# A decoder layer on one core: weight-quadrant sums by accumulating DMA, the last adaLN split moved into the down projection, token sums on VectorE

## The chip, the cores and the metric

One Trainium2 chip, of which the program uses one core. The metric is device time of one execution in microseconds (us). Engines are named as in the profile: PE is TensorE (matmuls), PEld its weight loads, DVE is VectorE, ACT is ScalarE, POOL is GpSimd, SP is SyncE, which here only issues DMAs. ACT and POOL issue DMAs too, each on a queue of its own.

## The reference

One trunk layer for 512 tokens of width 2048, all in float32:

```python
mod = silu(c) @ w_ada + b_ada            # six vectors: sh_a, sc_a, gt_a, sh_f, sc_f, gt_f
h = rmsnorm(x, g_pre_attn) * (1 + sc_a) + sh_a
qa, ka, va, qb, kb, vb = split(h @ w_in, 6)
oa = rmsnorm(dilated_mixture_attention(rope(qa) * s, rope(ka), va), g_out_a)
ob = rmsnorm(differential_attention(rope(qb) * s, rope(kb), vb, lam), g_subln_b) * (1 - lambda_init)
x = x + gt_a * rmsnorm(concat(oa, ob) @ w_out, g_post_attn)
h = rmsnorm(x, g_pre_ffn) * (1 + sc_f) + sh_f
f = (silu(h @ w_gate) * (h @ w_up)) @ w_down        # width 5632
x = x + gt_f * rmsnorm(f, g_post_ffn)
```

`c` is one vector, so each of the six `w_ada` parts (2048 x 2048, 16 MB) is read once and reduced against `silu(c)`: pure transfer, and a product with a sum on VectorE.

## The kernel before, in words

**Steps.** The whole program is a list of steps, `steps`. A step is one weight tile of 128 x 1024 float32 (512 KB) and the matmuls that use it. To keep float32 accuracy the tile is split into a high part `w_hi` (ACT, L1530, `do_hi`) and a low part `w_lo` (DVE, L1539, `do_lo`), the activations likewise, and each product is three matmuls of 128x512 (L282 to L284: high x high, high x low, low x high). Splits run two steps ahead of the matmuls (`LA = 2`): in step i, ACT makes the high part of step i+2 and DVE its low part. There are three buffers for each. What else is due in a step hangs in tables keyed by step number (`start_ev`, `pe_ev`, `mid_ev`, `post_ev`, `post_late`, `post_end`, and `aux` for extra loads); the loop at the end emits them in that order, and every engine and every queue then runs its own instructions strictly in that order. Nothing reorders them afterwards.

**Loads.** SP loads weight tiles into a ring of four buffers, `w_raw` (`NRAW = 4`, `pump_loads`, L1515). The ring is shared: tiles of the steps and "aux" tiles of `w_ada` (`in_adar`) go through it in order of use, and a load is issued when the tile four places earlier has been used.

**Stages.** The input projection with attention; the output projection (64 steps from `W0`, 12 matmuls each, `in_wout`); block 0 of the FFN (32 steps from `F0`, `in_wgu`); blocks 1 to 10 of the FFN (280 steps from `F1`); the down projection (88 steps from `D0`, 24 matmuls each, `in_wdown`, with the activations read back from DRAM).

**The adaLN parts.** `w_ada` parts n = 2, 0, 1, 3 are each 32 tiles of 512 KB. A planner loop walks the steps, adds up estimated DVE and DMA time, and hangs as many tiles on each step as it thinks fit. `ada_use` does the work: one DVE instruction with an accumulated sum (L228) against `silu(c)`. Part 3 (`gt_f`) is needed last, at the end of the down projection, through `ada_row` (a transpose on PE, a small DMA out, and a broadcast back into `GTG[1]`).

**Blocks 1 to 10: seven products for eight.** For a block the gate and up weights form a 2 x 2 matrix of quadrants q0 to q3 (gate/up by halves of the input width), 4 tiles each. With sums of token halves ("E" tiles) and sums of quadrants, seven products of four steps replace eight: slots m1 (q0), P (q0+q2), Q (q0+q2+q3), Y2 (q3), R (q2+q3), m2 (q1), T (the rest). Step numbers inside a block run from 0 to 27: P at 4 to 7, Q at 8 to 11, Y2 at 12 to 15, R at 16 to 19, m2 at 20 to 23, T at 24 to 27. `w_load` (SP) loads every quadrant once, 16 tiles a block, and `w_sums` (DVE, L1379) makes the sums in place, 16 tile sums a block, four steps ahead of use (`SL = 4`). Twelve buffers hold these tiles; `w_free` and `w_sums` give them back.

**Token sums.** In block 0, from step F0+16, `e_load` (SP) reads eight pieces of the normalised activations back from DRAM; `e_sums` makes four sums of 128x256 for each on POOL (L1233 to L1236), and `e_split` copies the result to a high part on ACT (L1247) and the rest to a low part on DVE (L1248). The same piece of the program also ends the output projection's second half of tokens: residual, norm, and transposes back (`wo_res`, `wo_norm`, `h2_tr`, L1178 on PE).

**The end.** `d_evac` takes the down projection's sums out of PSUM: a square with a sum on ACT (L1476) and the product with `GTG[1]` on DVE (L1477).

The two lines around which the change turns are the planner's list and the place of its left-overs:

```python
ada_todo = [(n, ch, hf) for n in (2, 0, 1, 3) for ch in range(16) for hf in range(2)]
...
for i, (n, ch, hf) in enumerate(ada_todo):
    aux[D0 + 2 + i].append((adar[n, ch, hf], ada_use(n, ch, hf)))
```

Of the kernel before, what the change touches and what calls it, by code (L numbers as in the profile page):

```python
# [5 lines left out]
F = mybir.dt.float32  # L6
# [28 lines left out]
def body(tc, t):  # L35
# [5 lines left out]
    with ctx:  # L41
# [874 lines left out]
        rawt = {}  # L916
# [4 lines left out]
        for g in range(1, 11):  # L921
            for name, a, bk in SLOTS:
                for j in range(4):
# [11 lines left out]
                    quad = {"m1": 0, "P": 0, "Q": 0, "T": 0, "m2": 1, "R": 2, "Y2": 3}[name]  # L935
                    add("s", None, mm, prov=lambda g=g, quad=quad, j=j: rawt[g, quad, j])
# [95 lines left out]
        ada_todo = [(n, ch, hf) for n in (2, 0, 1, 3) for ch in range(16) for hf in range(2)]  # L1032
# [18 lines left out]
        for i in range(W0 + 60):  # L1051
# [24 lines left out]
            while ada_todo and (ada_todo[0][0] == 3 or i < W0 + 46) and i >= 1 and t_dve + 1.14 <= t_end + (M_ADA if i < W0 else M_ADAW) and \  # L1076
# [153 lines left out]
        def e_sums(j):  # L1230
            h, e = v3(esum[j], 4), stage.get()
            o = v3(e, 4)
            pool.tensor_tensor(o[:, 0, :], h[:, 2, :], h[:, 3, :], op=OP.subtract)  # L1233
            pool.tensor_tensor(o[:, 1, :], o[:, 0, :], h[:, 0, :], op=OP.subtract)
            pool.tensor_tensor(o[:, 2, :], h[:, 0, :], h[:, 2, :], op=OP.subtract)
            pool.tensor_tensor(o[:, 3, :], h[:, 1, :], o[:, 1, :], op=OP.add)  # L1236
            stage.add(esum[j])
            esum[j] = e

        def e_split(j):  # L1240
# [4 lines left out]
            o = v3(esum[j], 4)  # L1245
# [82 lines left out]
        post_ev[F0 + 8].append(lambda: stage_alloc(0))  # L1328
# [14 lines left out]
        SL = 4  # L1343
# [412 lines left out]
```

## Time and profile before

| | us |
|---|---|
| median of 3 runs | 2279.52 |
| range of the runs | 2278.01 to 2283.3 |
| the profiled execution, its own time | 2278.92 |
| its span, first to last instruction | 2277.1 |
| PE busy | 2222.8 (98%) |
| DVE busy | 1594.9 (70%) |
| ACT busy | 1032.8 (45%) |
| POOL busy | 74.2 (3%) |
| mean granted TensorE clock | 0.992 |

A matmul of 128x512 is shown with 0.39 us, but in a full stretch one starts every 0.227 us: they overlap in the pipeline. So a gap of up to some 0.16 us between two of them does not show as idle time, and time lost in a stage is better read from the number of matmuls in a stretch than from PE's busy share. The profiled execution is 0.6 us below the median of the runs.

### The profile page before, as it was taken

How to read it: one execution, taken by the hardware profiler on the slowest of the kernel's cores; microseconds unless marked ns; L12 is line 12 of the kernel's file. 1: busy time of each engine (PE TensorE's matmuls, PEld its weight loads, DVE VectorE, ACT ScalarE, POOL GpSimd, SP SyncE). 2: the span in 40 equal slices, each digit the busy share in tenths (PEclk: the TensorE clock that was granted, in tenths of full speed). 3: DMA queues.
4: the chain of work that ended last, by engine and by line, in shares of the span. 5: the costliest groups of instructions: out<-in, count | busy, mean ns of one | idle time of the engine just before them, and what ended most of it. 6: DMA issues, size and time to landing. Idle time of an engine off the chain costs nothing.

```text
span 2277.1 us, 26712 instructions
## 1 busy us (share of the span) xinstructions
PE 2222.8 (98%) x10012; PEld 1808.3 (79%) x10012; DVE 1594.9 (70%) x2201; ACT 1032.8 (45%) x1507; POOL 74.2 (3%) x68
## 2 busy tenths in 40 slices
PE   7999999999999888999999999999999999999998
PEld 6888777778887666778888888888888888888886
DVE  6987877776777786777778777777777644444445
ACT  5443344444435454644454444444444433333432
POOL 0000000000001000150000000000000000000000
PEclk8999999999999999999999999999999999999999
DMA  9796544456778888864224323422432656655564
GB/s 370 296 332 213 157 139 166 145 163 192 222 260 278 300 295 300 276 240 147 94 93 157 130 98 115 157 93 93 157 140 80 252 194 211 195 189 200 189 218 185
DMA packets 124802, 440.11 MB, mean 193 GB/s; under 512 B 13792, under 2 KB 25344, under 8 KB 118272
## 3 DMA queue, kind: packets, MB, share of 16 engines
q1 hardware_dynamic: 105936, 406.14, 51.8%
q10 hardware_dynamic: 18736, 32.27, 4.4%
q8 instruction: 78, 1.28, 0.2%
q14 instruction: 52, 0.43, 0.1%
HBM read 404.25 MB, written 25.18 MB: 189 GB/s over the span
## 4 chain that ended last, share of the span: by engine, by line
PE 83%; DMA 6%; DVE 6%; issue 2%; ACT 2%; POOL 1%; ACTq 0%; SPq 0%; DVEq 0%; POOLq 0%
PE b L283 21%; PE b L284 21%; PE b L282 20%; PE b L277 5%; PE b L279 5%; PE b L278 5%; DMA w_raw<-in_wout 5%; DVE w_lo L1539 2%; PE b L507 2%; PE b L545 1%; ACT w_hi L1530 1%; DVE w_raw L228 1%; PE b L1262 1%; PE b L500 1%; PE b L529 1%
## 5 line engine op out<-in xcount | busy, mean ns | idle before, releaser
L1539 DVE TENSOR_TENSOR w_lo<-w_raw,w_hi 128x1024 fp32r<-128x1024 f32 x264 | 325.6, 1237 | 312.9 <-ACT w_hi L1530 312.5
L1530 ACT ACTIVATE w_hi<-w_raw 128x1024 fp32r<-128x1024 f32 x264 | 278.7, 1057 | 461.6 <-PE b L284 309.2
L283 PE MATMUL b<-w_lo,h 128*128 128x512 f32 x864 | 338.6, 392 | 7.7 <-DVE w_lo L1539 6.2
L282 PE MATMUL b<-w_hi,h 128*128 128x512 f32 x864 | 342.1, 396 | 0.4 <-ACT xT L212 0.4
L284 PE MATMUL b<-w_hi,h 128*128 128x512 f32 x864 | 337.1, 390 | 0.0
L1530 ACT ACTIVATE w_hi<-raw 128x1024 fp32r<-128x1024 f32 x196 | 208.1, 1062 | 268.9 <-PE b L284 244.3
L1539 DVE TENSOR_TENSOR w_lo<-raw,w_hi 128x1024 fp32r<-128x1024 f32 x196 | 240.1, 1229 | 103.1 <-ACT w_hi L1530 102.6
L284 PE MATMUL b<-w_hi,acthl 128*128 128x512 f32 x704 | 274.0, 389 | 0.4 <-DVE acthl L972 0.4
L282 PE MATMUL b<-w_hi,acthl 128*128 128x512 f32 x704 | 274.1, 389 | 0.0
L283 PE MATMUL b<-w_lo,acthl 128*128 128x512 f32 x704 | 273.9, 389 | 0.0
L282 PE MATMUL b<-w_hi,e 128*128 128x512 f32 x640 | 249.7, 390 | 0.0
L283 PE MATMUL b<-w_lo,e 128*128 128x512 f32 x640 | 249.0, 389 | 0.0
L284 PE MATMUL b<-w_hi,e 128*128 128x512 f32 x640 | 249.0, 389 | 0.0
L277 PE MATMUL b<-h,w_hi 128*128 128x512 f32 x512 | 213.4, 417 | 0.0
L278 PE MATMUL b<-h,w_hi 128*128 128x512 f32 x512 | 201.0, 393 | 1.6 <-DVE h L273 1.6
L279 PE MATMUL b<-h,w_lo 128*128 128x512 f32 x512 | 201.6, 394 | 0.0
L283 PEld LDWEIGHTS b<-w_lo,h 128*128 128x128 f32 x864 | 162.3, 188 | 48.1 <-DVE w_lo L1539 15.0
L282 PEld LDWEIGHTS b<-w_hi,h 128*128 128x128 f32 x864 | 162.2, 188 | 37.5 <-issue 3.7
L284 PEld LDWEIGHTS b<-w_hi,h 128*128 128x128 f32 x864 | 162.2, 188 | 33.6
L284 PEld LDWEIGHTS b<-w_hi,acthl 128*128 128x128 f32 x704 | 132.1, 188 | 28.0 <-DVE acthl L972 0.8
L282 PEld LDWEIGHTS b<-w_hi,acthl 128*128 128x128 f32 x704 | 132.1, 188 | 27.8 <-DVE stage L1314 0.2
L283 PEld LDWEIGHTS b<-w_lo,acthl 128*128 128x128 f32 x704 | 132.2, 188 | 27.3
(246 smaller groups left out, 3262.8 us busy)
## 6 DMA issues: line engine op xcount, KB each, us to landing
w_raw<-in_adar SPq DMA_DIRECT2D x128, 512.0 KB, 4.6
raw<-in_wgu SPq DMA_DIRECT2D x109, 512.0 KB, 4.5
w_raw<-in_win SPq DMA_DIRECT2D x107, 512.0 KB, 5.0
actf<-act2d SPq DMA_DIRECT2D x88, 512.0 KB, 4.7
w_raw<-in_wdown SPq DMA_DIRECT2D x88, 512.0 KB, 3.5
w_raw<-in_wout SPq DMA_DIRECT2D x64, 512.0 KB, 4.9
w_lent<-in_wgu SPq DMA_DIRECT2D x51, 512.0 KB, 4.6
ada<-in_ada SPq DMA_DIRECT2D x21, 1024.0 KB, 9.2
```

Of the source, the lines that this page charges most:

```text
L228: dve.scalar_tensor_tensor(w, w, 1.0, silu_h[half], op0=OP.mult, op1=OP.mult, accum_out=dst)
L277: pe.matmul(ps, whi, ahi, start=start, stop=False, **kw)
L278: pe.matmul(ps, whi, alo, start=False, stop=False, **kw)
L279: pe.matmul(ps, wlo, ahi, start=False, stop=stop, **kw)
L282: pe.matmul(ps, ahi, whi, start=start, stop=False, **kw)
L283: pe.matmul(ps, ahi, wlo, start=False, stop=False, **kw)
L284: pe.matmul(ps, alo, whi, start=False, stop=stop, **kw)
L500: pe.matmul(sc[:, r], qk[:, i, qs], qk[:, i + 1, :N], start=True, stop=True)
L507: pe.matmul(sc[:, :N], qk[k, 2 * m, qs], qk[k, 2 * m + 1, :N], start=True, stop=True)
L529: pe.transpose(tr[:, j, :], misc["p"][:, n % 2, 128 * j:128 * j + 128], ident)
L1530: act.activation(hi, raw, AF.Copy)
L1539: dve.tensor_tensor(lo, raw, hi.bitcast(F), op=OP.subtract)
```

## The change

Six things, all in the tables and helpers named above:

1. **Quadrant sums.** `w_load` now loads five sets a block: q2 as "P", q0 as "B11", q3 as "B22", q2 again as "R", q1 as "B21", 20 tiles. `w_sums` makes three of the four sums with DMAs issued by POOL that add what they read to what lies in the buffer (`accum_op=OP.add`): P += q0, later P += q1, and R += q3, 12 a block. One sum, P += B22, stays on DVE, 4 a block. Buffers are given back after m1, Y2, R, m2 and T.
2. **The last adaLN part.** The planner no longer places part 3. All its 32 tiles hang on down-projection steps D0+2 to D0+33. `ada_row(3)` moves from D0+18..20 to D0+34..36, and the spill of `silu(c)` from W0+62 to W0+50.
3. **Its consumer.** `d_evac` of the first column group copies instead of multiplying by `GTG[1]`; `d_gain` multiplies later, at D0+46, 48, 50, 52.
4. **Token sums.** `e_sums` runs on DVE instead of POOL, with the high-part copy on ACT right behind it; the low part (`e_lo`) is made one step later. The eight pieces stand 2.5 steps apart instead of 2, from F0+17 to F0+34.
5. **Transposes** (`h2_tr`) of both token halves run one step later.
6. **Buffers.** The first stage buffers of block 0 are taken at F0+2 instead of F0+8, and three of the four lent buffers at F1-4 instead of F1-3.

```diff
@@ planner
-        ada_todo = [(n, ch, hf) for n in (2, 0, 1, 3) for ch in range(16) for hf in range(2)]
+        ada_todo = [(n, ch, hf) for n in (2, 0, 1) for ch in range(16) for hf in range(2)]
...
-        assert len(ada_todo) <= 16 and all(a[0] == 3 for a in ada_todo), ada_todo
-        start_ev[W0 + 62].append(lambda: [act.dma_start(silud[:, 1024 * h:1024 * h + 1024], silu_h[h]) for h in range(2)])
+        assert not ada_todo
+        ada_todo = [(3, ch, hf) for ch in range(16) for hf in range(2)]
+        start_ev[W0 + 50].append(lambda: [act.dma_start(silud[:, 1024 * h:1024 * h + 1024], silu_h[h]) for h in range(2)])
...
-        row = ada_row(3, 7)
-        post_late[D0 + 18].append(row[0])
-        mid_ev[D0 + 19].insert(0, row[1])
-        start_ev[D0 + 20].append(row[2])
+        row = ada_row(3, 3)
+        post_late[D0 + 34].append(row[0])
+        mid_ev[D0 + 35].insert(0, row[1])
+        start_ev[D0 + 36].append(row[2])
@@ token sums
-            pool.tensor_tensor(o[:, 0, :], h[:, 2, :], h[:, 3, :], op=OP.subtract)
...
+            dve.tensor_tensor(o[:, 0, :], h[:, 2, :], h[:, 3, :], op=OP.subtract)
...
+            act.activation(SA["E", 0, j // 2][:, j % 2], o, AF.Copy)
+        def e_lo(j):
             hi, lo = SA["E", 0, j // 2][:, j % 2], SA["E", 1, j // 2][:, j % 2]
-            act.activation(hi, o, AF.Copy)
-            dve.tensor_tensor(lo, o, hi.bitcast(F), op=OP.subtract)
+            dve.tensor_tensor(lo, v3(esum[j], 4), hi.bitcast(F), op=OP.subtract)
...
         for j in range(8):
-            post_ev[F0 + 16 + 2 * j].append(lambda j=j: e_load(j))
-            post_ev[F0 + 17 + 2 * j].append(lambda j=j: e_sums(j))
-            post_ev[F0 + 19 + 2 * j].append(lambda j=j: e_split(j))
+            at = F0 + 17 + 5 * j // 2
+            start_ev[at - 3].append(lambda j=j: e_load(j))
+            post_end[at].append(lambda j=j: e_sums(j))
+            post_end[at + 1].append(lambda j=j: e_lo(j))
@@ quadrant sums and loads
-        def w_sums(e):
-            p = e + SL
...
-            ab = {"P": (0, 2), "Q": (0, 3), "R": (2, 3), "T": (0, 1)}.get(name)
...
-            dve.tensor_tensor(x, x, y, op=OP.add)
...
-        wloads = sorted((F1 + 28 * (g - 1) + {0: -2, 2: 0, 3: 4, 1: 18}[q] + j, g, q, j)
-                        for g in range(1, 11) for q in range(4) for j in range(4))
-        LEAD = 4
+        wloads = sorted((F1 + 28 * (g - 1) + at + j, F1 + 28 * (g - 1) + end + j, g, n, q, j)
+                        for g in range(1, 11) for n, q, at, end in
+                        (("P", 2, -8, -5), ("B11", 0, -6, -4), ("B22", 3, -1, 2), ("R", 2, 6, 9), ("B21", 1, 14, 16))
+                        for j in range(4))
+        USE.update({"m1": "B11", "P": "P", "Q": "P", "Y2": "B22", "R": "R", "m2": "B21", "T": "P"})
...
+        def w_sums(e):
+            for g in range(1, 11):
+                k = e - F1 - 28 * (g - 1)
+                for j in range(4):
+                    if k - j == -4:
+                        pool.dma_start(rawt[g, "P", j], wgu[g, 0, j], accum_op=OP.add)
+                    elif k - j == 4:
+                        dve.tensor_tensor(rawt[g, "P", j], rawt[g, "P", j], rawt[g, "B22", j], op=OP.add)
+                    elif k - j == 7:
+                        pool.dma_start(rawt[g, "P", j], wgu[g, 1, j], accum_op=OP.add)
+                    elif k - j == 10:
+                        pool.dma_start(rawt[g, "R", j], wgu[g, 3, j], accum_op=OP.add)
...
@@ transposes (both token halves)
-            pe_ev[b1 + 8 + i].append((0, a))
-            post_ev[b1 + 8 + i].append(b)
+            pe_ev[b1 + 9 + i].append((0, a))
+            post_ev[b1 + 9 + i].append(b)
...
@@ end
-            dve.tensor_tensor(u, ps, GTG[1][:, cg, :], op=OP.mult)
+            if cg == 0:
+                dve.tensor_copy(u, ps)
+            else:
+                dve.tensor_tensor(u, ps, GTG[1][:, cg, :], op=OP.mult)
+        def d_gain(tb):
+            u = HF["du", tb][:, 0, :]
+            dve.tensor_tensor(u, u, GTG[1][:, 0, :], op=OP.mult)
...
```

**SP's queue, output projection.** `in_wout` is a step's weight tile, `in_adar` a tile of `w_ada`, `in_xtok` the tokens for the residual. Before, around the first pair of token loads:

```order
L1515 DMA w_raw<-in_adar 128x1024
L1515 DMA w_raw<-in_wout 128x1024 x2
L1128 DMA x_5898<-in_xtok 128x2048
L1128 DMA x_5900<-in_xtok 128x2048
L1515 DMA w_raw<-in_adar 128x1024
L1515 DMA w_raw<-in_wout 128x1024
```

Now, from the last `in_adar` of this stage on:

```order
L1522 DMA w_raw<-in_adar 128x1024
L1522 DMA w_raw<-in_wout 128x1024 x9
L1128 DMA x_5889<-in_xtok 128x2048
L1128 DMA x_5891<-in_xtok 128x2048
L1522 DMA w_raw<-in_wout 128x1024 x32
L1128 DMA x_6642<-in_xtok 128x2048
L1128 DMA x_6644<-in_xtok 128x2048
L1522 DMA w_raw<-in_wout 128x1024 x6
```

Of the 49 tiles of `w_ada` that stood between the first and the last `in_wout` load, 19 are left, all ahead of the 18th `in_wout` load; the 30 behind it, two for every three weight tiles, are gone to the down projection.

**POOL's queue, one block of the FFN, now** (L1395 is P += q1, L1397 is R += q3, L1391 is the next block's P += q0; the buffers are `raw` and `w_lent`). Before, POOL had nothing here:

```order
L1395 DMA raw_7682<-in_wgu 128x1024
L1395 DMA raw_7683<-in_wgu 128x1024
L1395 DMA w_lent<-in_wgu 128x1024
L1397 DMA raw_7683<-in_wgu 128x1024
L1395 DMA w_lent<-in_wgu 128x1024
L1397 DMA raw_7419<-in_wgu 128x1024
L1397 DMA w_lent<-in_wgu 128x1024
L1397 DMA raw_7682<-in_wgu 128x1024
L1391 DMA raw_7683<-in_wgu 128x1024
```

The first of R's four sums stands fourth, behind three of P's; the last stands eighth.

**DVE, block 0, two pieces of token sums, now** (`w_lo` is a step's low part, L1233 to L1236 the sums that were POOL's, L1246 the low part of a token sum):

```order
L1546 TENSOR_TENSOR w_lo<-w_raw,w_hi 128x1024
L1233 TENSOR_TENSOR stage_7304<-stage_6928 128x256
L1234 TENSOR_TENSOR stage_7304<-stage_7304,stage_6928 128x256
L1235 TENSOR_TENSOR stage_7304<-stage_6928 128x256
L1236 TENSOR_TENSOR stage_7304<-stage_6928,stage_7304 128x256
L1546 TENSOR_TENSOR w_lo<-w_raw,w_hi 128x1024
L1246 TENSOR_TENSOR e_7337<-stage_7304,e_7333 128x1024
L1546 TENSOR_TENSOR w_lo<-w_raw,w_hi 128x1024
L1233 TENSOR_TENSOR stage_7304<-stageb 128x256
```

The four sums now stand between two low parts; before, DVE had only `w_lo` (two in a row) and the low part of a token sum here.

## Rows read from the trace of the kernel before

**Rows 1.** The page, part 1: busy time, share of the span, instructions.

```profile
PE 2222.8 (98%) x10012; PEld 1808.3 (79%) x10012; DVE 1594.9 (70%) x2201; ACT 1032.8 (45%) x1507; POOL 74.2 (3%) x68
```

**Rows 2.** Stretches: us; busy (x) of PE, PEld, DVE, ACT, POOL; PEclk, DMA share, GB/s.

```profile
676.80:734.80 58.00, 55.29 (x290) 46.25 (x289) 45.62 (x82) 30.16 (x66) 7.29 (x4) 1.00 0.83 281
734.80:903.70 168.90, 146.36 (x609) 113.61 (x608) 124.38 (x175) 77.52 (x117) 3.69 (x4) 0.96 0.86 306
903.70:950.00 46.30, 46.20 (x217) 37.40 (x216) 38.48 (x55) 35.12 (x55) 4.65 (x4) 1.00 0.77 257
950.00:1004.00 54.00, 47.78 (x209) 37.98 (x209) 34.16 (x28) 26.10 (x28) 33.02 (x30) 1.00 0.76 285
1004.00:1787.20 783.20, 781.84 (x3514) 645.75 (x3514) 600.69 (x543) 377.99 (x429) 4.69 (x3) 1.00 0.35 121
1787.20:2268.50 481.30, 480.93 (x2130) 397.78 (x2128) 226.29 (x211) 185.37 (x209) 1.66 (x3) 1.00 0.61 205
```

**Rows 3.** The same view, a stretch inside the down projection.

```profile
1860.00:2260.00 400.00, 399.63 (x1764) 330.48 (x1763) 182.06 (x165) 154.61 (x173) 0.55 (x1) 1.00 0.58 196
```

**Rows 4.** Waits, 734 to 904 us: total us, times, longest us.

```profile
ACT w_hi L1530 <- DMA w_raw<-in_wout: 69.3, 32, 6.7
...
PE b L283 <- DVE w_lo L1539: 12.7, 15, 2.5
...
PE b L1178 <- DVE x L1156: 3.7, 1, 3.7
```

**Rows 5.** Chain that ended last, 735 to 770 us: start us, us, what.

```profile
756.04 8.35 DMA w_raw<-in_wout
...
766.84 4.61 DMA w_raw<-in_adar
```

**Rows 6.** Groups of instructions, 950 to 1009 us (second half of block 0).

```profile
L1539 DVE TENSOR_TENSOR w_lo<-w_raw,w_hi 128x1024 fp32r<-128x1024 f32 x16 | 23.0, 1454 | 4.0 <-ACT w_hi L1530 4.0
...
L1247 ACT ACTIVATE e<-stage 128x1024 fp32r<-128x1024 f32 x7 | 7.4, 1058 | 13.0 <-POOL stage L1236 13.0
...
L1233 POOL TENSOR_TENSOR stage<-stageb 128x256 f32<-128x256 f32 x3 | 4.9, 1641 | 2.7 <-DMA stageb<-h2d 2.7
...
L1235 POOL TENSOR_TENSOR stageb<-stage 128x256 f32<-128x256 f32 x1 | 0.7, 744 | 0.0
```

**Rows 7.** The same view, whole span.

```profile
L1530 ACT ACTIVATE w_hi<-raw 128x1024 fp32r<-128x1024 f32 x196 | 208.1, 1062 | 268.9 <-PE b L284 244.3 <-DVE w_lo L1539 6.9 <-DVE stage L1318 5.0
...
L1379 DVE TENSOR_TENSOR raw<-raw,raw 128x1024 f32<-128x1024 f32 x62 | 76.0, 1226 | 0.0
...
L843 DVE TENSOR_TENSOR mixlo<-mixT,mixhi 128x256 fp32r<-128x256 f32 x32 | 12.1, 421 | 13.3 <-ACT mixhi L842 13.3
```

**Rows 8.** Timeline, ACT, then DVE, block 0: start us, us, what.

```profile
963.69 1.06 ACT L1247 ACTIVATE e<-stageb 128x1024 fp32r<-128x1024 f32 x1 [0.62 <-POOL stage L1233]
964.65 1.04 ACT L1530 ACTIVATE w_hi<-w_raw 128x1024 fp32r<-128x1024 f32 x1
...
968.89 1.21 DVE L1248 TENSOR_TENSOR e<-stage,e 128x1024 fp32r<-128x1024 f32 x1
970.03 1.21 DVE L1539 TENSOR_TENSOR w_lo<-w_raw,w_hi 128x1024 fp32r<-128x1024 f32 x1
```

**Rows 9.** Chain that ended last, blocks 1 and 2.

```profile
1075.32 1.24 DVE stage L1306
...
1153.70 1.24 DVE stage L1306
```

**Rows 10.** DMA issues: count, KB each, median us from issue to landing.

```profile
w_raw<-in_adar SPq DMA_DIRECT2D x128, 512.0 KB, 4.6
raw<-in_wgu SPq DMA_DIRECT2D x109, 512.0 KB, 4.5
...
ada<-in_ada SPq DMA_DIRECT2D x21, 1024.0 KB, 9.2
```

**Rows 11.** DMA rate in 40 slices of 735 to 904 us.

```profile
GB/s 355 219 305 143 382 420 410 281 282 309 283 333 257 253 288 205 354 354 391 340 241 267 279 306 320 320 190 247 378 172 276 259 425 411 273 305 315 334 381 359
```

More of the change, by code (lines that the diff above doesn't have):

```diff
@@ L934, in mm @@
                                  first and k == 0, j == 3 and k == 1, skip_group_check=True)
-                    quad = {"m1": 0, "P": 0, "Q": 0, "T": 0, "m2": 1, "R": 2, "Y2": 3}[name]
-                    add("s", None, mm, prov=lambda g=g, quad=quad, j=j: rawt[g, quad, j])
+                    add("s", None, mm, prov=lambda g=g, name=name, j=j: rawt[g, USE[name], j])
         D0 = len(steps)
@@ L1075, in body @@
             t_dma = max(t_dma, t_pe) + 1.45 * (1 + len(aux[i]))
-            while ada_todo and (ada_todo[0][0] == 3 or i < W0 + 46) and i >= 1 and t_dve + 1.14 <= t_end + (M_ADA if i < W0 else M_ADAW) and \
+            while ada_todo and i < W0 + 46 and i >= 1 and t_dve + 1.14 <= t_end + (M_ADA if i < W0 else M_ADAW) and \
                     t_dma + 1.45 <= t_end + M_DMA and len(aux[i]) < NAUX:
@@ L1232, in e_sums @@
             o = v3(e, 4)
-            pool.tensor_tensor(o[:, 0, :], h[:, 2, :], h[:, 3, :], op=OP.subtract)
-            pool.tensor_tensor(o[:, 1, :], o[:, 0, :], h[:, 0, :], op=OP.subtract)
-            pool.tensor_tensor(o[:, 2, :], h[:, 0, :], h[:, 2, :], op=OP.subtract)
-            pool.tensor_tensor(o[:, 3, :], h[:, 1, :], o[:, 1, :], op=OP.add)
+            dve.tensor_tensor(o[:, 0, :], h[:, 2, :], h[:, 3, :], op=OP.subtract)
+            dve.tensor_tensor(o[:, 1, :], o[:, 0, :], h[:, 0, :], op=OP.subtract)
+            dve.tensor_tensor(o[:, 2, :], h[:, 0, :], h[:, 2, :], op=OP.subtract)
+            dve.tensor_tensor(o[:, 3, :], h[:, 1, :], o[:, 1, :], op=OP.add)
             stage.add(esum[j])
             esum[j] = e
-        def e_split(j):
             if ("E", 0, 0) not in SA:
@@ L1389, in w_load @@
+        USE.update({"m1": "B11", "P": "P", "Q": "P", "Y2": "B22", "R": "R", "m2": "B21", "T": "P"})
         def w_load(e):
-            while wloads and wloads[0][0] - LEAD <= e:
-                need_, g, q, j = wloads[0]
-                p = rawp.get(("R2", "R8", "P1", "P4") if g == 10 and q < 2 else None)
+            while wloads and wloads[0][0] <= e:
+                at, end, g, n, q, j = wloads[0]
+                p = rawp.get(("R2", "R8", "P1", "P4") if g == 10 and n in ("P", "B21") else None)
@@ L1393, in w_load @@
                 if p is None:
-                    assert need_ > e + 1, (need_, e, g, q, j)
+                    assert end > e, (e, wloads[0])
                     return
                 wloads.pop(0)
-                rawp_of[g, q, j] = p
-                rawt[g, q, j] = p[1]
+                rawp_of[g, n, j] = p
+                rawt[g, n, j] = p[1]
                 sync.dma_start(p[1], wgu[g, q, j])
+        def w_sums(e):
[10 more added lines that the diff above has]
+                        pool.dma_start(rawt[g, "R", j], wgu[g, 3, j], accum_op=OP.add)
@@ L1406, in w_free, with raw_lend @@
                 k, j = divmod(r, 4)
-                if SLOTS[k][0] in ("R", "T"):
-                    rawp.add(rawp_of.pop((g + 1, 2 if SLOTS[k][0] == "R" else 0, j)))
+                if SLOTS[k][0] not in ("P", "Q"):
+                    rawp.add(rawp_of.pop((g + 1, USE[SLOTS[k][0]], j)))
         actu = []
-        def raw_lend():
-            for _ in range(4):
+        def raw_lend(n):
+            for _ in range(n):
                 w = wp.tile([128, 1024], F, name="w_lent", tag="raw", bufs=NRAW)
@@ L1461, in body @@
             a, b = h2_tr(1, i, 4 + i % 4)
-            pe_ev[b1 + 7 + i].append((0, a))
-            post_ev[b1 + 7 + i].append(b)
+            pe_ev[b1 + 8 + i].append((0, a))
+            post_ev[b1 + 8 + i].append(b)
         out = t["out"]
@@ L1642, in body @@
             k = i - D0 - 66
+            if i - D0 in (46, 48, 50, 52):
+                d_gain((i - D0 - 46) // 2)
             if k in (10, 12, 14, 16):
```

20 lines of the change are left out of this document (4 added, 16 removed).

## Prediction

> **What bounds the kernel now.** I read the busy times first: PE is busy for 98% of the span [rows 1], so only a stretch in which PE waits can give time back. Next the table of stretches, one per stage [rows 2]. In the down projection PE starts 1764 instructions in 400.0 us, one per 0.227 us [rows 3]; that is my price of a 128x512 matmul at the full clock (granted 1.00, the 2.4 GHz level). A step of 12 matmuls then takes 2.72 us, a step of 24 takes 5.45. In block 0 the stretch 903.7 to 950 holds 217 instructions, 30 of them short transposes (of 128 columns): 187 x 0.227 = 42.4, and 3.9 us for the 30, 0.13 each. With these two prices I ask of each stretch what PE alone would need:
>
> - 734.8 to 903.7 (output projection, steps 16 to 63): 577 x 0.227 + 32 x 0.13 = 135.1 of 168.9 us. **34 us lost**, and the mean clock is 0.96.
> - 676.8 to 734.8 (steps 0 to 15): by the same count some 4 us lost.
> - 950 to 1004 (rest of block 0, 8 transposes): 201 x 0.227 + 1.0 = 46.6 of 54.0. **7 us lost.**
> - 1004 to 1787 (blocks 1 to 10): a block takes 78.4 us from one L1306 to the same one of the next block [rows 9]. Its matmuls take 336 x 0.227 = 76.3, its 16 transposes 2.1: under 1 us a block is lost.
> - The down projection: nothing, 481 us for 88 x 5.45 = 480.
>
> So two stretches can give, by 34 and 7 us. In the first, the waits say what ends last [rows 4]: ACT waited 69.3 us in 32 pieces for `in_wout` tiles, and PE then for the parts made from them. The chain shows the same, tile after tile landing 4.6 to 8.4 us after its issue [rows 5]. The ring of four buffers is the bound: a load is issued when the tile four places earlier is used, and here five tiles in every three steps go through it. DMA engines are not full (share 0.86, 306 GB/s [rows 2], with slices of 420 [rows 11]).
>
> **The change, part by part.**
>
> *30 `w_ada` tiles leave the output projection.* From step 15 on one tile per step goes through the ring instead of 5/3. The ring turned over 113 tiles in the 226.9 us of this stage, 2.0 us each; one per 2.72 us is within that. VectorE also loses 30 products of 1.2 us. What is then late next: residual and norm around step 39, where PE once waited 3.7 us for L1156 [rows 4]. The same work for the other token half ran in block 0, 903.7 to 950, without `w_ada` tiles, and there PE was busy for 46.2 of 46.3 us [rows 2]; the change also gives it one more step. I keep 1.5 us of the 34 as a remainder: **-32.5 us.** Ends: -34 (all of it) and -22.5 (only what PE's busy column shows idle, 168.9 - 146.4).
>
> *The 32 tiles in the down projection.* Per step of 5.45 us the ring now takes two tiles, 2.73 us each, against 2.0 shown possible. VectorE adds 1.2 us to the 2.6 it is busy per step (226 us in 88 steps), ACT nothing. DMA goes from 205 GB/s to 205 + 0.52 MB / 5.45 us = 301 for 174 us, under the 306 of the stage they leave. Cover: the split runs two steps ahead, so a tile may be 5 us late before PE sees it. **0.** Upper end: 1.1 us a tile, what each costs now (34 / 30), 36 us in all. If the cover went, PE would wait for `w_lo`.
>
> *Gate row, gains, spill.* The row moves 16 steps; a bank of the first column group is free by then. Four gains of 128x512 on VectorE are hidden by its idle half. The spill of `silu(c)` on ACT's queue stands ahead of nothing that is due. 0.
>
> *Token sums on VectorE.* POOL needed 1.6 us for a sum beside VectorE and 0.74 alone; `w_lo` took 1454 ns on average there, against 1226 for a like instruction in the later blocks [rows 7]; ACT waited 13.0 us for POOL [rows 6]. Now a piece costs VectorE 4 x 0.42 [rows 7] and no waiting for POOL. But in both queues new waits stand in line: ACT's copy waits for the sums, and the next `w_hi` stands behind it. One round is `w_lo` 1.23, sums 1.7, copy 1.06, `w_hi` 1.06 [rows 7], `w_lo` 1.23 = 6.3 us, in 2.5 steps = 6.8 us: it fits, but where a piece comes after two steps (5.45 us), or where block 0's two sigmoids (step 25) fall in, the part is late. Followed piece by piece with the full durations I lose 13.6 us, with starts as close as the trace shows them in a row (0.96 us on ACT, 1.14 on DVE [rows 8]) 6.6 us, against 7 now. **0**, ends -4 and +6.
>
> *Quadrant sums by DMA.* VectorE loses 12 of 16 sums of 1.23 us a block [rows 7], worth nothing here: PE did not wait for it. L1306 waits for ACT's sigmoid, which stands behind `w_hi`, not for a sum. The price is in what replaces them. A block now moves 32 tile transfers instead of 16: 16.8 MB in 78.4 us, 214 GB/s instead of 107, plus 13 GB/s of stores; under 306. 12 of them add to their destination, and the trace has no such transfer. Two of the three have time: the next block's P has 10 steps, T some 15. R is the tight one. POOL's first sum into P waits until VectorE has made Q's first `w_lo` (end of step 6); R's last stands eighth in POOL's queue, and must have landed 2.3 us (1.06 + 1.23) before step 19: 12 x 2.72 - 2.3 = 30 us for eight. Less 5 us of DMA time for the four B21 loads behind them, **3.2 us each** may be spent. Bounds for one: 1.25 us (0.52 MB at the 420 GB/s of a slice [rows 11]) and 4.5 us (a plain load from issue to landing [rows 10], if they ran strictly one after another); the far end is 9.2, the landing of a transfer of twice the bytes in the crowded start [rows 10]. The program lets eight be in flight, so I take the near end: hidden, **0**.
> The Trainium skill (Collectives: The Full Stack, "The bandwidth ceiling") says that a reducing transfer is slower not for its add but because it reads two sources, which halves its rate. No row here shows it; by it one would take 2.5 us, an estimate, still under 3.2, and the sum stays, with a third of the margin.
>
> **Sum.** 2278.9 (the profiled execution) - 32.5 + 0 = 2246.4; that execution lies 0.6 below the median, so **2247 us**.
>
> **Rivals.**
>
> 1. *The accumulating DMA is late (slower).* Place: R's sums, steps 16 to 19 of each block: ACT's `w_hi` waits for a POOL transfer, PE for both. For it: there is no row for such a transfer, eight stand in one queue, and the eighth is due. Against: 30 us of cover, and DMA engines with a share of 0.35 there [rows 2]. Over 3.2 us each, a block loses 8x + 5 - 30.4 us; the whole gain is spent at x = 3.6. At 4.5 us: 10.6 us a block, 106 in all: 2247 + 106 = **2353**.
> 2. *The stall moves with the tiles.* The down projection waits for its ring as the output projection did: half of 36 us comes back, **2265**; all of it, 2283, no change. Against it: two tiles in 5.45 us where the ring did 2.7.
> 3. *The output projection does not let go.* Another chain (norms, PSUM evacuation) takes the place of the ring and only the lower end is gained: 2278.9 - 22.5 + 0.6 = **2257**. Against it: the clean stretch 903.7 to 950.
>
> **How the numbers follow.** My forecast 0.61, its own range 2236 to 2256. Rival 3, 0.10; rival 2, 0.10, of it 0.04 without change; rival 1, 0.19. A measurement of this kernel can tell about 0.2% (4.6 us) from no change. Faster: 0.61 + 0.10 + 0.06 = 0.77; same 0.04; slower 0.19. The range has to hold 8 in 10. Low end: all 34, the 7 of block 0 and 3 in blocks 1 to 10 gained: 2278.9 - 44 = 2235. High end: rivals 2 and 3 whole, and rival 1's start: 2285. Beyond it lies most of rival 1.
>
> **What would show it.** Right: the output projection from its step 16 takes 136 us, no ACT wait for `in_wout` over a few us, clock 1.00 there; L1306 to the next still 78.4 us; the down projection 481 us with L228 in it and no PE wait; block 0 near 100 us, ACT waiting for the sums on DVE instead of POOL. Wrong: ACT waits for a DMA `raw<-in_wgu` issued by POOL around R, a block well over 79 us, or landing times of these transfers over some 10 us.

## The result and the profile after

| | before | after |
|---|---|---|
| median, us | 2278.77 (4 runs, 2276.07 to 2283.3) | 2250.15 (4 runs, 2247.42 to 2250.81) |
| ratio, 95% interval | | 0.987 [0.9852, 0.9888] |
| span of the profiled execution | 2277.1 | 2248.8 |

The change is faster by 28.6 us (2247 was forecast, within 2235 to 2285). Where it comes from is read stage by stage, from the start of a stage's first matmul to the start of the next stage's first (the down projection: to the start of its last), as the timelines of TensorE give them. All kernels of this study stand in one table (us; "a later block" is the usual period of blocks 2 to 10):

| kernel | output projection | block 0 | block 1 | a later block | down projection | median |
|---|---|---|---|---|---|---|
| before | 226.9 | 100.4 | 78.4 | 78.4 | 480.3 | 2278.8 |
| **after** | **192.6** | **99.2** | **86.0** | **78.3** | **480.4** | **2250.2** |
| 1 adaLN part alone | 194.1 | 100.5 | 78.3 | 78.4 | 480.3 | 2245.9 |
| 2 quadrant sums back on DVE | 192.6 | 97.3 | 84.0 | 78.4 | 480.6 | 2248.8 |
| 3 transfers without the add | 193.2 | 96.2 | 83.0 | 78.3 | 480.3 | 2245.3 |
| 4 q1's two steps later | 191.7 | 97.4 | 85.6 | 78.3 | 480.3 | 2250.6 |
| 5 R's first | 192.5 | 97.2 | 85.8 | 78.3 | 480.3 | 2249.2 |
| 6 R's twice | 193.3 | 97.5 | 98.4 | 90.6 (mean) | 480.3 | 2371.5 |
| 7 two adaLN tiles a step | 193.1 | 97.3 | 87.4 | 78.3 | 480.3 | 2249.3 |
| 8 = 2, sums on POOL, copy two steps on | 192.5 | 92.7 | 78.3 | 78.4 | 480.3 | 2237.9 |
| 9 = 2, sums on DVE, copy two steps on | 194.0 | 92.7 | 78.6 | 78.4 | 480.3 | 2237.1 |
| 10 = after, copy two steps on | 193.1 | 92.7 | 84.0 | 78.3 | 480.3 | 2242.1 |
| 11 = 1, with 30 products | 200.5 | 100.6 | 78.4 | 78.4 | 480.3 | 2253.4 |
| 12 = before, part 3 in half tiles | 218.2 | 100.2 | 78.4 | 78.4 | 480.3 | 2269.6 |

Each row is one profiled execution, and a stage whose code is the same in two kernels can differ between them: the output projection takes 191.7 to 194.1 us in the changed kernel and experiments 1 to 10, and experiment 7, which differs from the changed kernel in the down projection alone, has 97.3 and 87.4 for blocks 0 and 1 instead of 99.2 and 86.0. Differences of a stage under some 2 us are not read as effects.

So 34.3 us were gained in the output projection and 1.2 in block 0, and 7.6 given back in block 1. The busy times of the page, part 1, against [rows 1]:

```profile
PE 2214.3 (98%) x10012; PEld 1807.1 (80%) x10012; DVE 1471.7 (65%) x2117; ACT 1030.5 (46%) x1507; POOL 142.7 (6%) x156
```

VectorE lost 123 us of work, net, mostly quadrant sums, and that is no measure of anything: the later blocks that they left take 78.3 us instead of 78.4. The stretches of the changed kernel (columns as in [rows 2]): output projection steps 16 to 63, block 0 by halves, block 1, blocks 2 to 10, down projection.

```profile
734.30:868.90 134.60, 134.60 (x610) 111.06 (x609) 89.69 (x115) 77.38 (x117) 3.69 (x4) 1.00 0.79 268
868.90:917.10 48.20, 48.11 (x225) 38.85 (x224) 38.86 (x56) 35.55 (x55) 4.66 (x4) 1.00 0.75 244
917.10:968.10 51.00, 48.26 (x201) 38.85 (x200) 36.54 (x50) 23.08 (x25) 2.80 (x3) 0.93 0.84 287
968.10:1054.10 86.00, 80.62 (x354) 64.14 (x352) 51.79 (x53) 38.69 (x43) 11.49 (x13) 1.00 0.91 264
1054.10:1759.10 705.00, 704.22 (x3171) 581.81 (x3169) 421.68 (x380) 340.28 (x390) 91.87 (x104) 1.00 0.81 223
1759.10:2239.70 480.60, 480.23 (x2124) 397.10 (x2122) 262.20 (x274) 184.80 (x209) 1.66 (x3) 1.00 0.70 238
```

In the first row PE is busy for all of 134.60 us at a granted clock of 1.00, where [rows 2] had 146.36 of 168.90 at 0.96. The third and fourth are what is left: PE idle for 2.7 and 5.4 us, the clock at 0.93 in the third. In blocks 2 to 10 the DMA share rose from 0.35 to 0.81 and PE did not notice. The waits of the first stretch, against [rows 4] (L1537 is now the line of `w_hi`, L1546 that of `w_lo`):

```profile
ACT w_hi L1537 <- PE b L284: 41.2, 34, 1.7
...
ACT w_hi L1537 <- DMA w_raw<-in_wout: 9.6, 4, 3.6
...
PEld b L283 <- DVE w_lo L1546: 0.4, 2, 0.2
```

ACT's wait for `in_wout` is down from 69.3 us to 9.6; it now waits for PE to free a buffer, so PE is the bound.

What the new transfers cost stands in two places. The page, part 3 (queue; packets, MB, share of 16 engines' span), and the instructions of L1397, the sums into R (first who waited for them, then issue to landing):

```profile
q1 hardware_dynamic: 111696, 427.11, 54.6%
q0 software_dynamic: 17280, 62.92, 14.7%
```

```profile
  ACT w_hi L1537: 67.9, 26
...
DMA to landing us min/median/max: 8.3/15.4/22.0
```

q0 holds the 120 accumulating transfers: 14.7% of 2248.8 us over 120 is 2.75 us of all 16 engines for each 512 KB. R's forty, which stand behind others, land after 15.4 us in the median, and ACT waited 67.9 us for them. Block 4 shows how near that came (timelines of ACT, DVE, PEld and PE; R's last tile):

```profile
1261.17 1.06 ACT L1537 ACTIVATE w_hi<-w_lent 128x1024 fp32r<-128x1024 f32 x1 [2.75 <-DMA w_lent<-in_wgu]
```

```profile
1262.26 1.23 DVE L1546 TENSOR_TENSOR w_lo<-w_lent,w_hi 128x1024 fp32r<-128x1024 f32 x1 [2.59 <-ACT w_hi L1537]
```

```profile
1263.54 0.19 PEld L283 LDWEIGHTS b<-w_lo,e 128*128 128x128 f32 x1 [0.16 <-DVE w_lo L1546]
```

```profile
1263.64 0.39 PE L283 MATMUL b<-w_lo,e 128*128 128x512 f32 x1
```

The low part is done between 1263.40, where DVE's next instruction starts, and 1263.49. The matmul starts at 1263.64, in its turn, but its weight load already had to wait 0.16 us for the low part: nothing was left in hand. In block 2 the low part was ready 0.9 us before the matmul. In block 1 the cover did not suffice. PE waited at steps 18 and 19, which took 3.33 and 3.80 us instead of 2.72, 1.7 us in all (timeline of PE, step 19):

```profile
1028.53 0.50 PE L283 MATMUL b<-w_lo,e 128*128 128x512 f32 x1 [0.76 <-DVE w_lo L1546]
```

### The profile page after: what moved, and what is told of

It is laid out like the page before. It is cut to its first block, busy times and chain, and to the rows that moved or that the text cites. A ratio compares the mean times of both kernels' runs of the same rounds, so it can differ in the third digit from the quotient of the medians.

```text
span 2248.8 us, 27045 instructions
## 1 busy us (share of the span) xinstructions
PE 2214.3 (98%) x10012; PEld 1807.1 (80%) x10012; DVE 1471.7 (65%) x2117; ACT 1030.5 (46%) x1507; POOL 142.7 (6%) x156
## 3 DMA queue, kind: packets, MB, share of 16 engines
q0 software_dynamic: 17280, 62.92, 14.7%
## 4 chain that ended last, share of the span: by engine, by line
PE 90%; DVE 4%; DMA 3%; issue 1%; ACT 1%; POOL 0%; SPq 0%; ACTq 0%; DVEq 0%; POOLq 0%
PE b L283 23%; PE b L284 23%; PE b L282 23%; PE b L277 5%; PE b L279 5%; PE b L278 5%; PE b L507 2%; DMA w_lent<-in_wgu 2%; DVE w_lo L1546 1%; PE b L545 1%; PE b L529 1%; PE b L1260 1%; PE b L500 1%; ACT w_hi L1537 1%; DMA w_raw<-in_wout 1%
## 5 line engine op out<-in xcount | busy, mean ns | idle before, releaser
L1546 DVE TENSOR_TENSOR w_lo<-w_raw,w_hi 128x1024 fp32r<-128x1024 f32 x264 | 321.9, 1222 | 280.3 <-ACT w_hi L1537 280.1
L1537 ACT ACTIVATE w_hi<-w_raw 128x1024 fp32r<-128x1024 f32 x264 | 278.3, 1057 | 424.0 <-PE b L284 333.2
L1546 DVE TENSOR_TENSOR w_lo<-raw,w_hi 128x1024 fp32r<-128x1024 f32 x189 | 230.5, 1223 | 186.6 <-ACT w_hi L1537 185.7
L1537 ACT ACTIVATE w_hi<-raw 128x1024 fp32r<-128x1024 f32 x189 | 200.1, 1060 | 256.9 <-PE b L284 190.0
L278 PE MATMUL b<-h,w_hi 128*128 128x512 f32 x512 | 200.5, 392 | 3.0 <-DVE h L273 3.0
L283 PEld LDWEIGHTS b<-w_lo,h 128*128 128x128 f32 x864 | 163.1, 189 | 45.1 <-DVE w_lo L1546 11.7
L1546 DVE TENSOR_TENSOR w_lo<-w_lent,w_hi 128x1024 fp32r<-128x1024 f32 x91 | 111.1, 1223 | 88.0 <-ACT w_hi L1537 87.7
L1537 ACT ACTIVATE w_hi<-w_lent 128x1024 fp32r<-128x1024 f32 x91 | 96.5, 1060 | 131.0 <-PE b L284 97.3
L284 PEld LDWEIGHTS b<-w_hi,acthl 128*128 128x128 f32 x704 | 132.2, 188 | 28.4 <-DVE acthl L971 0.8
```

Source lines behind the costliest of these rows:

```text
L278: pe.matmul(ps, whi, alo, start=False, stop=False, **kw)
L283: pe.matmul(ps, ahi, wlo, start=False, stop=False, **kw)
L284: pe.matmul(ps, alo, whi, start=False, stop=stop, **kw)
L1537: act.activation(hi, raw, AF.Copy)
L1546: dve.tensor_tensor(lo, raw, hi.bitcast(F), op=OP.subtract)
```

## The experiments

Each kernel is compared with the kernel before on the same chip; medians of before were 2280.1 (runs 1 to 4), 2279.5 (5 to 8) and 2279.7 us (9 to 12).

**1. The adaLN part alone.** Only the edits to the planner, `ada_row(3)`, the spill, `d_evac` and `d_gain`:

```diff
-        ada_todo = [(n, ch, hf) for n in (2, 0, 1, 3) for ch in range(16) for hf in range(2)]
+        ada_todo = [(n, ch, hf) for n in (2, 0, 1) for ch in range(16) for hf in range(2)]
```

> The kernel before with only the last adaLN part moved into the down projection (with its row, its gains and the spill of silu(c)); token sums stay on POOL, all quadrant sums on VectorE. Theory (the moved tiles are the whole gain): the output projection takes 192.6 us as in the changed kernel (226.9 before), the down projection 480, block 0 stays near 100.4, all ten later blocks at 78.4: 2278.8 - 34.3 = 2244.5 us, 2241 to 2248, so about 6 us faster than the full change. Rival (the other parts bring something too): slower than the full change, above 2252.

Measured: 2245.94, ratio 0.9855 [0.9841, 0.987]. As the theory had it: 32.8 us from the output projection, all else as before. By the medians the other parts together cost some 4 us; the two intervals overlap, but the slowest of these four runs (2246.7) is faster than the changed kernel's fastest (2247.42).

**2. Quadrant sums back on VectorE.** `w_load`, `w_sums`, `w_free` and `raw_lend` as before, the rest as changed.

> The changed kernel with the quadrant sums and their loads put back as before (16 sums a block on VectorE, 16 loads); token sums stay on VectorE. Theory (the extra transfers at the start of block 1 cost its 7.6 us): block 1 returns from 86.0 to 78.4 us, block 0 stays near 99.2 with 5 us lost at its step 27: 2250.2 - 7.6 = 2242.6, 2240 to 2246. Rival (the token sums on VectorE, whose last pieces fall in block 1's first steps, cost it): block 1 stays above 84, 2250.

Measured: 2248.76, ratio 0.9869 [0.9851, 0.9886]. The theory fell: block 1 only went from 86.0 to 84.0. Most of its loss, which sits in steps 4 and 5 here, does not need the new transfers; experiment 9 shows what it comes from.

**3. The same transfers without the add.**

```diff
-                        pool.dma_start(rawt[g, "R", j], wgu[g, 3, j], accum_op=OP.add)
+                        pool.dma_start(rawt[g, "R", j], wgu[g, 3, j])
```

(likewise for the two sums into P)

> The changed kernel with the twelve DMAs a block plain, on the same queue: they overwrite the buffer, so three of the four quadrant sums are left out. Theory (the add itself doubles what a transfer takes on the DMA engines): q0 falls from 2.75 us of all 16 engines per 512 KB transfer to about 1.4, ACT's wait for R's tiles (67.9 us in 26 pieces) falls under 10 us, block 1 loses 2 to 5 us instead of 7.6: 2245 to 2248. Rival (the software queue of POOL is slow whatever it carries): 2.5 us or more per transfer, waits and time unchanged, 2250.

Measured: 2245.29, ratio 0.9854 [0.9838, 0.9869]. Page, part 3 and 6 (issues: count, KB, median us to landing), and L1397:

```profile
q0 software_dynamic: 17280, 62.92, 8.2%
...
raw<-in_wgu SPq DMA_DIRECT2D x133, 512.0 KB, 4.5
```

```profile
DMA to landing us min/median/max: 4.3/6.1/11.0
```

8.2% of 2242.8 us over 120 transfers is 1.53 us: the add makes 2.75 of it, 1.8 times, and nobody waits for L1397 any more. The plain loads beside them land in 4.5 us, as in [rows 10], where the changed kernel shows 8.8. The Trainium skill (Collectives: The Full Stack, "The bandwidth ceiling") says of a collective's reducing step that its two source reads, and not the add, halve its rate. The factor of 1.8 here is near that; what the engines read, no run here shows. Block 1 still takes 83.0, about as in experiment 2, which has no such transfers.

**4. Later, on paper.** The point was to use up the last cover of R's transfers.

```diff
-                    elif k - j == 7:
+                    elif k - j == 9:
                         pool.dma_start(rawt[g, "P", j], wgu[g, 1, j], accum_op=OP.add)
```

> The changed kernel with the sums P += q1 issued two steps later (9 instead of 7), so that the run of eight accumulating transfers with R's among them starts 5.4 us later. Theory (2.75 us per transfer: eight and the plain loads beside them fill the DMA engines up to 0.1 to 1.0 us before PE needs R's last low part): 4.4 to 5.3 us lost in each of ten blocks, block period 82.5 to 83.7, 2294 to 2303 us. Rival (1.25 us per transfer as the prediction took: 15 us of cover left): nothing lost, 2250.

Measured: 2250.6, ratio 0.9872 [0.9856, 0.9889]: no change, but this does not speak for the rival. The edit did not delay anything: in blocks 2, 4 and 5 the first of these sums was issued 20.4 us into the block in both kernels. POOL has no other work there, so the step in the table sets only the order in its queue; what sets the time is the data, which is VectorE's low part of Q (POOL waited 33 us for it in both kernels). The edit put R's transfers between P's, and ACT's wait for them fell to 28.2 us in 9 pieces.

**5. R's transfers first.**

```diff
-                    elif k - j == 7:
+                    elif k - j == 14:
```

> The changed kernel with R's four accumulating transfers queued ahead of P's second four (P += q1 moved from 7 to 14 in the table). Theory (R's wait is the place of its transfers in POOL's queue, behind four others of 2.75 us): ACT's wait for R's tiles falls from 67.9 us to under 10, block 1 loses nothing at its steps 18 and 19 (1.7 before); blocks 2 to 10 stay at 78.3; 2248 to 2250, not to be told from the change. Rival (P's second four, now behind, are late for T, or crowd the loads of B21): a period over 79, above 2257.

Measured: 2249.23, ratio 0.9863 [0.9846, 0.9879]. L1397 lands in 8.1 us, and nobody waits for it:

```profile
DMA to landing us min/median/max: 5.8/8.1/11.5
```

The wait in front of R was the place behind P's four. In blocks 2 to 10 it had been covered, and they are as before. In block 1 it had not: steps 18 and 19 now take 2.72 us each. Block 1 as a whole is still at 85.8, because its step 1 took 5.1 us here against 4.2, and the total cannot be told from the change.

**6. R's transfers twice,** the suspected cost doubled:

```diff
+                for j in range(4 if k == 13 else 0):
+                    pool.dma_start(rawt[g, "R", j], wgu[g, 3, j], accum_op=OP.add)
```

> The changed kernel with each of R's four accumulating transfers issued a second time (q3 is added twice, so R's products are not the reference's): 16 accumulating transfers a block, 12 of them in the run that ends with R's last. Theory (2.75 us of all DMA engines each, 0.1 to 1.0 us of cover left): four more cost 10 to 11 us in each of ten blocks, period 88 to 89, 2350 to 2360. Rival (several us of cover are left, or the transfers overlap better than their DMA time says): less than 4 us a block, under 2290.

Measured: 2371.47, ratio 1.0403 [1.0388, 1.0419]: 12.3 us per block, a little over the theory's 10 to 11. Waits of 1055 to 1880 us, and two stretches of block 2:

```profile
POOL raw L1399 <- DMA raw<-in_wgu: 83.9, 22, 6.9
PE b L282 <- ACT w_hi L1539: 80.6, 9, 10.3
```

```profile
1112.00:1118.00 6.00, 0.00 (x0) 0.00 (x0) 0.00 (x0) 0.16 (x1) 0.87 (x1) 0.50 1.07 258
1118.00:1124.00 6.00, 4.58 (x10) 3.30 (x11) 3.74 (x5) 3.01 (x3) 0.00 (x0) 0.50 1.05 225
```

PE waits some 9 us in each of blocks 2 to 10 (10.3 at most) for R, as rival 1 of the prediction has it, only for its first tile and not its last. The DMA engines are full (share 1.05), and after the wait the granted clock is 0.50 (1.2 GHz), which adds to the bill; so do the second transfers, each of which has to wait until the first into its buffer has landed (L1399 is the added line). Four more transfers decide between nothing and some 120 us.

**7. Two adaLN tiles a step in the down projection.**

```diff
-            aux[D0 + 2 + i].append((adar[n, ch, hf], ada_use(n, ch, hf)))
+            aux[D0 + 2 + i // 2].append((adar[n, ch, hf], ada_use(n, ch, hf)))
```

> The changed kernel with two tiles of the last adaLN part on each of the down projection's steps 2 to 17 instead of one on each of steps 2 to 33: three tiles per 5.45 us through the ring, 385 GB/s with the activations. Theory (the ring turns a tile every 2.0 us, as in the output projection of the kernel before): 6.0 us of tiles per step, 0.55 x 16 = 9 us less up to 5 us of cover lost in the down projection: 484 to 490 instead of 480.4, 2254 to 2259. Rival A (the DMA rate is the bound, and 385 GB/s is under it): 480, 2250. Rival B (1.1 us per extra tile, as the output projection paid): 16 tiles more than shown, 498, 2267.

Measured: 2249.29, ratio 0.9865 [0.985, 0.988], the down projection at 480.3. Its steps 1 to 17:

```profile
1765.00:1855.00 90.00, 90.00 (x402) 74.63 (x402) 69.02 (x88) 31.76 (x33) 0.00 (x0) 1.00 0.96 353
```

353 GB/s at a DMA share of 0.96, and PE busy for 90.00 of 90.00 us. Rival A: the 2.0 us a tile that the prediction read from the output projection is not what the ring can do at most; here it did three in a step of 5.45, one in 1.82.

**8 and 9. Token sums with the copy two steps behind,** on POOL and on VectorE. Base is experiment 2; both have this edit, and 8 also `pool` for `dve` in the four sums:

```diff
-            act.activation(SA["E", 0, j // 2][:, j % 2], o, AF.Copy)
         def e_lo(j):
             hi, lo = SA["E", 0, j // 2][:, j % 2], SA["E", 1, j // 2][:, j % 2]
+            act.activation(hi, v3(esum[j], 4), AF.Copy)
             dve.tensor_tensor(lo, v3(esum[j], 4), hi.bitcast(F), op=OP.subtract)
-            post_end[at + 1].append(lambda j=j: e_lo(j))
+            post_end[at + 2].append(lambda j=j: e_lo(j))
```

> The kernel of the second experiment (sums of quadrants on VectorE) with the token sums back on POOL, but a piece every 2.5 steps as in the change instead of every 2, and its high and low parts two steps behind. Theory (POOL needs 6.4 us for a piece beside VectorE, which fits 6.8 us and did not fit 5.45; no sums stand between two low parts on VectorE): block 0 loses under 3 us in its second half (7.9 with ada alone), block 1 under 1: 2240 to 2243, faster than all so far. Rival (ACT's copy waits for POOL all the same): as with ada alone, 2246.

> The kernel of the eighth experiment (sums of quadrants on VectorE, token sums a piece every 2.5 steps, high and low part two steps behind the sums) with the four sums of a piece on VectorE instead of POOL. Theory (what cost time in the change is not VectorE's work but ACT's copy right behind the sums, with the next w_hi behind it): no loss in block 0's second half and block 1 at 78.3, as with POOL: 2237 to 2239. Rival (the sums between two low parts on VectorE make w_lo late wherever the copy stands): 5 us or more lost in block 0 and block 1, 2243 to 2249.

Measured: 2237.93, ratio 0.9814 [0.9799, 0.9829], and 2237.1, ratio 0.9813 [0.9796, 0.9829]: both faster than all else here, with block 0 at 92.7 and block 1 at 78.3 and 78.6. The second half of block 0 with POOL, and then with VectorE:

```profile
916.90:961.40 44.50, 44.50 (x202) 36.89 (x201) 34.58 (x27) 24.75 (x26) 33.17 (x27) 1.00 0.87 320
```

```profile
917.80:962.20 44.40, 44.40 (x201) 36.87 (x200) 36.89 (x52) 24.80 (x26) 0.00 (x0) 1.00 0.86 321
```

PE is busy all the time in both, so with this spacing the engine that makes the sums does not matter. Experiments 2 and 9 differ only by where a piece's parts are taken: the copy moves from right behind the sums to two steps behind, and the low part with it from one step to two. That is worth 11.7 us; the two moves were not tried apart. How it costs so much is seen in the changed kernel, block 0, step 27 (timeline of ACT, then DVE):

```profile
946.70 1.06 ACT L1243 ACTIVATE e<-stage 128x1024 fp32r<-128x1024 f32 x1 [4.08 <-DVE stage L1236]
947.66 1.04 ACT L1537 ACTIVATE w_hi<-w_raw 128x1024 fp32r<-128x1024 f32 x1
948.61 1.06 ACT L1278 ACTIVATE stage<-b 128x512 f32<-128x512 f32 x2
```

```profile
946.25 0.42 DVE L1236 TENSOR_TENSOR stage<-stage,stage 128x256 f32<-128x256 f32 x1
949.22 1.28 DVE L1279 TENSOR_TENSOR stage<-stage,b 128x512 f32<-128x512 f32 x2 [2.56 <-ACT stage L1278]
950.42 1.22 DVE L1546 TENSOR_TENSOR w_lo<-w_raw,w_hi 128x1024 fp32r<-128x1024 f32 x1
```

ACT stands 4.08 us for the sums with the next `w_hi` behind it; then block 0's sigmoid (L1278) follows on ACT, DVE stands 2.56 us for that, and only then makes the low part. PE (timeline, then stretches):

```profile
951.70 0.80 PE L283 MATMUL b<-w_lo,h 128*128 128x512 f32 x1 [2.44 <-DVE w_lo L1546]
...
952.71 0.63 PE L282 MATMUL b<-w_hi,h 128*128 128x512 f32 x1
953.14 0.63 PE L283 MATMUL b<-w_lo,h 128*128 128x512 f32 x1
```

```profile
946.00:948.00 2.00, 2.00 (x11) 1.65 (x10) 0.66 (x2) 1.30 (x2) 0.00 (x0) 1.00 1.02 416
...
952.00:954.00 2.00, 2.00 (x6) 1.54 (x6) 2.00 (x3) 0.00 (x0) 0.40 (x1) 0.50 0.52 55
954.00:960.00 6.00, 6.00 (x20) 4.79 (x19) 3.89 (x7) 2.01 (x2) 0.00 (x0) 0.67 0.99 294
```

After a wait of 2.44 us the granted clock is 0.50, and matmuls start 0.43 us apart (952.71, 953.14) instead of 0.227. The step lost 5.1 us, of which the pause is some 2.7 (948.76 to 951.70, less 0.227) and the slower matmuls the rest. In block 1 of the same kernel PE waited up to 1.3 us at a time, and the granted clock stayed at 1.00. In experiment 9 block 0 has no such wait.

**10. The changed kernel with the copy two steps behind.** The same edit as in 9, on the changed kernel; against 9 it shows the quadrant transfers by themselves, against the change once more the place of the copy.

> The changed kernel with one thing different: ACT's copy of a token sum stands two steps behind the sums, with the low part, instead of right behind them. The quadrant sums stay with DMA, so against the ninth experiment it shows what these cost by themselves. Theory (quadrant sums by DMA are hidden once nothing else collides at the start of block 1): 2238 to 2240, block 1 at 78.3 to 80. Rival (the transfers crowd the start of block 1 on their own): block 1 over 82, 2242 or more.

Measured: 2242.11 (2241.76 to 2248.38), ratio 0.9842 [0.9827, 0.9857]. The rival: block 1 is at 84.0, and the median 5 us over experiment 9. Against the change 8.0 us are gained. Block 1's first three steps lose 6.5 us, against 0.8 in experiment 9; the chain that ended last leads there through a plain load of block 1's first product (start us, us, what):

```profile
950.38 15.51 DMA w_lent<-in_wgu
965.99 1.06 ACT w_hi L1537
967.08 1.24 DVE w_lo L1546
```

Issues of 942 to 972 us, here and then in experiment 9:

```profile
q0 software_dynamic: 432, 1.57, 26.7%
...
w_lent<-in_wgu SPq DMA_DIRECT2D x6, 512.0 KB, 15.4
```

```profile
w_lent<-in_wgu SPq DMA_DIRECT2D x4, 512.0 KB, 9.2
```

There the loads for P, for m1 and for the token sums and block 0's last tiles come together, and the adding transfers (1.57 MB) take 26.7% of all DMA time. Without the add this was not tried, so how much of the 5 us is the add and how much the additional bytes stays open.

**11 and 12. What held the output projection of before.** 11 adds 30 products to experiment 1 on tiles that lie there anyway (the spill of `silu(c)` back at W0+62); 12 halves the tiles of part 3, and the products made of them, in the kernel before.

```diff
+                if W0 + 16 <= i < W0 + 61 and i % 3:
+                    ada_dot(raw_, 0, red[:, 5, 0, 0:1])
```

```diff
-                sync.dma_start(w, src)
+                if it[0] == "a" and getattr(aux[it[1]][it[2]][1], "n", 0) == 3:
+                    sync.dma_start(w[:, 0:512], src[:, 0:512])
+                else:
+                    sync.dma_start(w, src)
```

> The first experiment's kernel (last adaLN part in the down projection) with 30 products of the same form (L228, 128x1024 with its sum) added on VectorE in the output projection's steps 16 to 60, two in every three steps, on tiles that are there anyway: VectorE's work of the kernel before without its 30 transfers. Theory (the ring of loads was the bound, not VectorE): output projection within 3 us of 194.1, total 2246 to 2249. Rival (the products delayed w_lo): 10 to 34 us come back, 2256 to 2280.

> The kernel before with the tiles of the last adaLN part halved: the same number of loads through the same ring at the same places, 256 KB instead of 512 KB each, with half of each product (half of that sum is left out). Theory (the ring's places bound it: a load waits for the use of the tile four places earlier): at least 20 of the 34 us stay lost, output projection 212 to 227, 2265 to 2279. Rival (bytes bound it: 30 x 0.26 MB less at 306 GB/s are 26 us): under 10 us stay lost, output projection 195 to 201, 2246 to 2254.

Measured: 2253.41, ratio 0.9882 [0.9867, 0.9897], and 2269.6, ratio 0.9959 [0.9945, 0.9974]. ACT's wait for `in_wout`, in 11 and in 12:

```profile
ACT w_hi L1539 <- DMA w_raw<-in_wout: 12.0, 4, 4.9
```

```profile
ACT w_hi L1537 <- DMA w_raw<-in_wout: 60.0, 30, 7.2
```

With half the bytes 24 of 33 us stay lost (218.2 against 194.1), and the wait is nearly that of [rows 4]: the places in the ring bind more than bytes. A half tile still keeps its place until it lands, 3.5 us in the median against 4.5 for a whole one. The half products that are left are part of the 24. The products alone give back 6.4 us, more than the theory's 3 and less than the rival's 10. They also keep a place in the ring 1.2 us longer, and this run cannot part the two. The shares (24, 9 and 6 of 33) are not a clean sum.

## Why the prediction was right

The forecast was 2247, the result 2250. Point by point:

- **30 tiles leave the output projection, -32.5:** measured -34.3 in the change and -32.8 alone, the same within the spread of this stage. Of the remainder of 1.5 us that was kept for the norm at step 39 little or nothing was needed: steps 16 to 63 take 134.6 us in the change and 135.8 alone, where the two prices of the prediction give 135.1. That the ring was the bound holds in the main (experiments 11 and 12): of 33 us, 9 went with half the bytes and half the products, and the products alone cost 6. Rival 3, with 22.5, is out.
- **Down projection, 0:** measured +0.1. The reason given was "2.73 us a tile against 2.0 shown possible"; experiment 7 shows 1.82 without loss, so the cover was larger than that. Rival 2 is out by more than the change needed.
- **Gate row, gains, spill, 0:** nothing seen.
- **Token sums on VectorE, 0 with ends -4 and +6:** measured +2.8 in the median (experiment 2 against 1, with the new spacing of the pieces). The named mechanism is the one that the trace shows: copy behind sums, `w_hi` behind copy, and the sigmoids of step 25. The value taken was too low, and it left out that the last pieces fall in block 1 and that the granted clock was 0.50 after PE's wait of 2.44 us. That POOL was slow beside VectorE was true and beside the point: with 2.5 steps a piece and the copy two steps behind, POOL does it without a loss (experiment 8).
- **Quadrant sums by DMA, 0:** this is the step that was mis-sized, twice. The near end, 1.25 us a transfer, was taken; measured 2.75, so of the 15 us that the near end would have left, under 1 us was left in blocks 2 to 10 and nothing in block 4. The Trainium skill's rule (Collectives: The Full Stack, "The bandwidth ceiling") gave an estimate of 2.5, which is near by two errors against each other: a plain transfer took 1.53 and not 1.25, and the factor was 1.8 and not 2. The cover of 30 us and the place (R's last tile, eighth in the queue) were right. The break-even of 3.2 us was too high: in block 4, between 1231.0 and 1261.2, the adding transfers took 74.2% of the DMA engines' time (22.4 us, 2.8 each) and plain ones 23.9%, which is 7.2 us where 5 were set aside, so that about 2.85 us each could be spent. That R's transfers stayed hidden there was luck: the price that said so was less than half of the real one. In block 1 of the change they were late by 1.7 us, which is rival 1 in small (not so in experiments 5 and 10, where steps 18 and 19 take 2.72), and experiment 6 shows it come true in full with four transfers more.
- **The same term at the start of block 1:** the count was made for a block in the middle. "The next block's P has 10 steps" does not hold for block 1, where P's loads and sums meet block 0's last loads: 5 us (experiment 10 against 9).

With 34.3 us gained in the output projection, 1.2 in block 0, 7.6 lost in block 1 and 0.4 gained elsewhere, the 28.3 us between the two spans are complete. Against the kernel before, blocks 0 and 1 together cost 6.4 us, and this sum hides two larger ones. Block 0 could be had in 7.7 us less (100.4 to 92.7 in experiment 9), and the two terms taken as nothing cost 13.1 us in the median against experiment 9. Together they cost less than singly (11.7 and 5.0, against the same kernel), probably because both fall in the first steps of block 1; that was not shown. That the forecast came within 3.2 us is in part luck: what these terms cost was made good in part by the 7.7 us, where the prediction had counted 7, and by 1.8 us more from the output projection than forecast.

What stays open: experiments 8 and 1 differ in the spacing of the pieces, the early buffers and the later transposes at once; which of them removes the 7.8 us that block 0 loses in experiment 1 (100.5 against 92.7) was not tried apart.

## What to carry to other kernels

Price a transfer that adds at nearly twice a plain one on the DMA engines, and look for its cost not only in the steady loop but at the loop's start, where its loads meet those of the stage before. Where an in-order engine has to take over another engine's result, put the taking two steps behind the making: the same work on the same engines was 11.7 us apart by that alone, and 8.0 with the quadrant sums by DMA. Work taken off an engine that is not waited for (123 us of VectorE here) is worth nothing until a wait names it.

## What was not expected of the hardware

- A transfer of 512 KB that adds to SBUF took 2.75 us of all 16 DMA engines against 1.53 without the add, and 872 ns of POOL's time to issue (L1395, median; 1.4 to 1.5 us for R's behind them) against 537; plain loads beside the adding ones landed after 8.8 us instead of 4.5.
- A pause of PE of 2.44 us was followed by matmuls at 0.43 us spacing, with a granted clock of 0.50 (1.2 GHz), until the stretch 954 to 960 (mean 0.67): the step lost 5.1 us, about twice the wait. Waits of up to 1.3 us in block 1 left the clock at 1.00.
- An engine that has only DMAs to issue runs ahead of the program's steps as far as its data lets it; moving its issues by two steps moved their order and not their time (experiment 4).
